# SSD mixer of a hybrid block: y summed in PSUM, squares reduced in one instruction, mask clamps and norm products moved

## The chip, the cores and the metric

The kernel runs on 1 core of one Trainium2 chip. The metric is device time in microseconds. The kernel before takes 1947.79 us, the median of 3 runs (1946.84 to 1948.59). Engines are named as in the profile: PE is TensorE, DVE is VectorE, ACT is ScalarE, POOL is GpSimd, SP is SyncE. ACT and SP also issue the DMA transfers that stand in their queues.

## What is computed

One decoder block on 1024 positions of 1024 channels, in float32: a projection `P = rmsnorm(x) @ W_in`, a gated short convolution, a Mamba-2 mixer (SSD, with 32 heads of 64 in 4 groups, chunks of 128 positions), a gated merge, and a convolutional MLP. The change lies in the SSD mixer:

```python
cb = einsum("bclgn,bcsgn->bcgls", cc, bc)
y_diag = einsum("bcgjls,bcsgjp->bclgjp", cb[:, :, :, None] * decay_in, x_)
y_off  = einsum("bclgn,bcgjpn,bcgjl->bclgjp", cc, prev, exp(a_cum))
y = y_diag + y_off + d_skip * xh
yf = y * silu(z)                                        # per group of 512 channels
yf = yf * rsqrt(mean(yf * yf, axis=-1) + EPS)           # then the norm's weight, W_s_out
```

`decay_in` is the exponential of differences of a cumulative sum, masked to the lower triangle.

## The kernel before

The large matrix products are made in pairs of column blocks, by a scheme of seven half-size products instead of eight (`Pair`, L274 on, and `then`, L368). Every operand is split into a rounded high part (`h_...`, an ACT cast, L146) and a low part (`l_...`, a subtraction on DVE or POOL, L147), so one half-size product is 12 matmuls of 128x512 on PE (`product`, L261, L268). A pair keeps one PSUM bank open through several of its products: after each, ACT copies the sum so far out (`u2...`, `u3...`, `cc`, L311 and L331), and only then may PE go on adding into that bank. `mark["act"]` holds the last such copy, `mark["pe"]` the last matmul of a product.

Beside the projection's pairs (`BESIDE`) runs the SSD mixer, from about 230 to 900 us of the span. Each finished product is a tick of a clock (`tick`, L394). `ssd_chunk` (L720) is a generator for one chunk of one group, 32 in all, started 6 ticks apart (`DSTEP`). `STAGES` says at which tick, counted from its diagonal block, each part of a chunk is written: loads (`m`, the rows of negated cumulative sums, and `in`, with x, B and C) at -9, the mask's clamps and exponential at -6 (`DECAY`, L742 and L743), transposes at -4 (`TRANS`, L748 to L770), z at -3, the diagonal block at 0 (`DIAG`, L788 to L821), squares at 3 (L824 to L828), the norm's product and, after each fourth chunk, its transpose at 6 (`NORM`, L831 to L844).

The names: `m` is first the load, then the mask (8 heads of 128x128), then mask times C·B (`pc`, in a bank of its own, made triangular into `cb`, L769, then L770 on DVE); `px` and `pb` hold x and B transposed; `bk` is ACT's copy of `pb` (L767); `pd` is the diagonal block, `po` the part from the carried state `st`, `pst` the new state; `xt` is x in the tile `in`, scaled by the skip on POOL (L763); DVE sums y in `xt` (L802, L805) and multiplies it into `zt` (L821). ACT squares `zt` into `eb` (L824); DVE adds the four blocks of 128 in two steps (L826, L828) into `ss`; PE sums over partitions (`pn`, L831), DVE scales (`yss`, L833), POOL takes the power -0.5 (`yr`, L837), and after four chunks PE transposes `yr` into `pr` (L841), ACT copies it to `rr` and SP stores it.

PSUM has 8 banks: four in rotation for `mm_tile` (the pairs' open sums) and four for `sd_tile`, which `px`, `pb`, `pc`, `pd`, `po`, `pst`, `pn`, `pr` and the pairs' second product `pb21` share. A tile taken from a rotation waits until the tile that had the bank four takings earlier has been read.

The order on each engine is not the order in which the code is written: a scheduler with a timeline of its own orders the instructions, and `tc.issue_after(i)` holds those written under it behind instruction `i`. The three engines' queues and the DMA queues then run in the order so fixed.

## Time and profile before

| | |
|---|---|
| median of 3 runs | 1947.79 us (1946.84 to 1948.59) |
| the profiled execution | 1947.18 us |
| its span, first to last instruction | 1945.5 us |
| PE busy | 1907.6 us (98%) |
| DVE busy | 1280.5 us (66%) |
| POOL busy | 1238.5 us (64%) |
| ACT busy | 958.6 us (49%) |
| mean granted PE clock | 0.995 of full speed |

The profile is of one execution. The span leaves out some 1.7 us around the program. PE is busy for all but 37.9 us of the span, so what counts is where PE stands idle and what ends each such wait; the share of busy time of the other engines says only how much room their queues have. A wait is put down to the instruction that came last.

### The profile page before, as it was taken

The numbers are of one execution on the slowest core, as the hardware profiler recorded it, in microseconds if no ns is written. First come the engines' busy times: TensorE is split into PE (matmuls) and PEld (weight loads), VectorE is DVE, ScalarE is ACT, GpSimd is POOL, SyncE is SP. The second block draws the span as 40 slices with busy tenths as digits, with TensorE's granted clock in tenths as the row PEclk, the third lists the DMA queues.
The fourth block names the chain that finished last, engine by engine and source line by source line (L and its number), as shares of the span: only waits on it lengthen the run. The fifth ranks groups of instructions, "written<-read, shape, count | busy, mean of one in ns | idle before, by whom it ended". The sixth has DMA issues, their size and how long they took to land.

```text
span 1945.5 us, 25405 instructions
## 1 busy us (share of the span) xinstructions
PE 1907.6 (98%) x8990; PEld 1567.3 (81%) x8990; DVE 1280.5 (66%) x1431; ACT 958.6 (49%) x1630; POOL 1238.5 (64%) x915
## 2 busy tenths in 40 slices
PE   8899999999999999999999999999999999999998
PEld 6788887787788778888888888887888888878886
DVE  9665567777786777777764833379655555675555
ACT  6347566667546754443542323454444444453334
POOL 8668766766767766766444534449867687754332
PEclk9999999999999999999999999999999999999999
DMA  4233354555545553443998974451332435487663
GB/s 157 87 95 134 132 168 147 179 158 164 184 138 160 170 166 124 149 144 122 386 368 275 358 253 164 160 178 65 109 114 76 128 131 174 143 290 257 203 195 141
DMA packets 180033, 337.90 MB, mean 174 GB/s; under 512 B 15265, under 2 KB 87745, under 8 KB 178882
## 3 DMA queue, kind: packets, MB, share of 16 engines
q1 hardware_dynamic: 93122, 253.43, 38.0%
q10 hardware_dynamic: 86784, 82.85, 13.2%
q8 instruction: 70, 1.15, 0.2%
q14 instruction: 57, 0.47, 0.1%
HBM read 246.82 MB, written 89.41 MB: 173 GB/s over the span
## 4 chain that ended last, share of the span: by engine, by line
PE 83%; DVE 5%; ACT 4%; DMA 3%; issue 3%; POOL 2%; ACTq 1%; SPq 0%; POOLq 0%; DVEq 0%
PE pb11up L268 9%; PE so L268 9%; PE pb11xb L268 6%; PE pt1up L268 5%; PE ya L268 5%; PE pb11cv L268 4%; PE pb11z L268 4%; PE d L1178 3%; PE d L1180 3%; PE d L1179 3%; PE pb21up L268 2%; PE pt1xb L268 2%; PE pb11ba L268 2%; PE pt1cv L268 2%; PE pt1g L268 2%
## 5 line engine op out<-in xcount | busy, mean ns | idle before, releaser
L618 DVE SCALAR_TENSOR_TENSOR cv<-xbc,scw,cv 128x1024 f32<-128x1024 f32 x72 | 121.9, 1696 | 42.4 <-ACT cv L614 41.1
L618 DVE SCALAR_TENSOR_TENSOR h<-fci,fcw,h 128x1024 f32<-128x1024 f32 x44 | 85.3, 1938 | 73.8 <-ACT h L614 73.2
L742 ACT ACTIVATE m<-m,tk 128x128 f32<-128x128 f32 x256 | 78.9, 390 | 87.3 <-DMA m<-acd 79.0
L147 POOL TENSOR_TENSOR l_ws<-raw_ws,h_ws 128x512 fp32r<-128x512 f32 x32 | 46.1, 1440 | 72.2 <-PE so L268 45.3
L146 ACT CAST h_ws<-raw_ws 128x512 fp32r<-128x512 f32 x64 | 39.8, 623 | 97.8 <-PE so L268 64.5
L268 PE MATMUL so<-yh,h_ws 128*128 128x512 f32 x256 | 69.0, 391 | 0.0
L268 PE MATMUL so<-yl,h_ws 128*128 128x512 f32 x256 | 68.6, 389 | 0.0
L268 PE MATMUL so<-yh,l_ws 128*128 128x512 f32 x256 | 68.5, 389 | 0.0
L146 ACT CAST h_wo<-raw_wo 128x512 fp32r<-128x512 f32 x48 | 29.7, 620 | 59.5 <-PE wo L1008 32.9
L147 DVE TENSOR_TENSOR l_ws<-raw_ws,h_ws 128x512 fp32r<-128x512 f32 x32 | 25.5, 796 | 50.9 <-PE so L268 21.4
L147 POOL TENSOR_TENSOR l_wo<-raw_wo,h_wo 128x512 fp32r<-128x512 f32 x24 | 31.7, 1322 | 39.4 <-PE wo L1008 31.3
L826 DVE TENSOR_TENSOR eb<-eb 128x256 f32<-128x256 f32 x32 | 27.4, 856 | 44.5 <-ACT eb L824 44.5
L268 PEld LDWEIGHTS so<-yh,l_ws 128*128 128x128 f32 x256 | 48.1, 188 | 10.0
L268 PEld LDWEIGHTS so<-yl,h_ws 128*128 128x128 f32 x256 | 48.1, 188 | 10.0
L268 PEld LDWEIGHTS so<-yh,h_ws 128*128 128x128 f32 x256 | 47.8, 188 | 9.6
L1155 DVE TENSOR_TENSOR h<-h 128x1024 f32<-128x1024 f32 x22 | 47.1, 2140 | 10.3 <-ACT h L1154 10.1
L314 DVE TENSOR_TENSOR fci<-fci,pb21up 128x512 f32<-128x512 f32 x18 | 12.4, 688 | 60.7 <-PE pb21up L268 60.7
L147 POOL TENSOR_TENSOR l_t3up<-raw_2up,h_t3up 128x512 fp32r<-128x512 f32 x22 | 31.2, 1418 | 32.1 <-PE pb11up L268 32.1
L1007 PE MATMUL wo<-l_wo,mh 128*128 128x512 f32 x128 | 50.0, 391 | 0.0
L1006 PE MATMUL wo<-h_wo,mh 128*128 128x512 f32 x128 | 50.0, 392 | 0.0
L1008 PE MATMUL wo<-h_wo,ml 128*128 128x512 f32 x128 | 49.7, 391 | 0.0
L770 DVE TENSOR_TENSOR m<-m,cb 128x1024 f32<-128x1024 f32 x32 | 48.6, 1518 | 0.6
(1127 smaller groups left out, 6527.8 us busy)
## 6 DMA issues: line engine op xcount, KB each, us to landing
m<-acd ACTq DMA_DIRECT2D x32, 512.0 KB, 3.9
raw_ws<-in_w_s_out SPq DMA_DIRECT2D x32, 512.0 KB, 4.7
ssd_in<-cv ACTq DMA_DIRECT2D x24, 512.0 KB, 2.9
in<-ssd_in ACTq DMA_DIRECT2D x32, 384.0 KB, 3.8
raw_wo<-in_w_o SPq DMA_DIRECT2D x24, 512.0 KB, 3.7
wd<-in_w_down SPq DMA_DIRECT2D x22, 512.0 KB, 7.0
td<-wd SPq DMA_DIRECT2D x44, 256.0 KB, 4.2
raw_2up<-in_w_up SPq DMA_DIRECT2D x22, 512.0 KB, 3.5
```

The source lines that it names most:

```text
L146: act.copy(hi, v)
L147: (eng or pool).tensor_tensor(lo, v, f32(hi), op=ALU.subtract)
L268: mark["pe"] = pe.matmul(ps, wt[:, k, :], ct[:, k, :], start=(start and n == 0), stop=(stop and n == 11), skip_group_check=held,).ins
L618: dve.scalar_tensor_tensor(cv, ci[:, j : j + SEQ], w[:, j : j + 1], cv, op0=ALU.mult, op1=ALU.add)
L742: act.activation(m[:, h, :], m[:, h, :], AF.Relu, bias=a)
L770: dve.tensor_tensor(m, m, cb.unsqueeze(1).to_broadcast([P, HG, P]), op=ALU.mult)
L1006: pe.matmul(pss[t], mh, wh, start=k == 0, stop=False)
L1007: pe.matmul(pss[t], mh, wl, start=False, stop=False)
L1008: pe.matmul(pss[t], ml, wh, start=False, stop=k == NK - 1)
L1178: pe.matmul(ps, aa[0][:, ts], bb[0], start=k == 0, stop=False)
L1179: pe.matmul(ps, aa[0][:, ts], bb[1], start=False, stop=False)
L1180: pe.matmul(ps, aa[1][:, ts], bb[0], start=False, stop=k == KF - 1)
```

## The change

- `y` is summed in the bank of its diagonal block, `pd += xt`, `pd += eb`, and read from there by `zt = pd * zt`. Before, it was summed in `xt`.
- `pb` and `pc` share one bank, `pbc`. The product with the triangle is made in place in it, and the mask is multiplied by it there. The tile `cb` is gone.
- One `tensor_reduce` over the four blocks takes the place of the two additions behind the square.
- The clamps and the exponential are written under `behind("act")`: on ACT they stand behind the pairs' last copy.
- The norm's product moves from tick 6 to 8, the power is taken once for four chunks, on 4 columns (8 instead of 32 instructions on POOL), and the transpose moves to tick 10. Both matmuls are written under `behind("pe")`.

```diff
@@ -49,7 +49,7 @@
 
 
 D0, DSTEP = 17, 6
-STAGES = LOAD_M, LOAD_IN, DECAY, TRANS, LOAD_Z, DIAG, SQUARES, NORM = -9, -9, -6, -4, -3, 0, 3, 6
+STAGES = LOAD_M, LOAD_IN, DECAY, TRANS, LOAD_Z, DIAG, SQUARES, NORM, ROW = -9, -9, -6, -4, -3, 0, 3, 8, 10
 
 
 AHEAD = 300
@@ -396,6 +396,13 @@
             clock[0] += 1
             for f in slots.pop(clock[0], ()):
                 f()
+
+    def behind(*engines):
+
+        held = ExitStack()
+        for e in engines:
+            held.enter_context(tc.issue_after(mark[e]))
+        return held
 
 
     xd_ = [dram.tile([P, 10, SEQ], F32, name=f"ssd_in{g}") for g in range(NG)]
@@ -737,18 +744,19 @@
         xt, bt, ct = inp[:, 0:4, :], inp[:, 4, :], inp[:, 5, :]
         yield
 
-        for h in range(HG):
-            a = tk[:, 0, cc, q, g * HG + h : g * HG + h + 1]
-            act.activation(m[:, h, :], m[:, h, :], AF.Relu, bias=a)
-        act.activation(m, m, AF.Exp, scale=-1.0)
+        with behind("act"):
+            for h in range(HG):
+                a = tk[:, 0, cc, q, g * HG + h : g * HG + h + 1]
+                act.activation(m[:, h, :], m[:, h, :], AF.Relu, bias=a)
+            act.activation(m, m, AF.Exp, scale=-1.0)
         yield
 
         px = sd_tile(f"px{nm}")
         for j in range(4):
             pe.transpose(px[:, j * P : (j + 1) * P], xt[:, j, :], ident)
-        pb = sd_tile(f"pb{nm}")[:, :P]
+        pbc = sd_tile(f"pbc{nm}")
+        pb, pc = pbc[:, :P], pbc[:, P : 2 * P]
         pe.transpose(pb, bt, ident)
-        pc = sd_tile(f"pc{nm}")[:, :P]
         pe.matmul(pc, bt, ct, start=True, stop=True)
         xd = c2(f"xd{nm}")
         dve.tensor_tensor(
@@ -765,9 +773,8 @@
         )
         bk = ssp.tile([P, P], F32, tag="bk", name=f"bk{nm}", bufs=1)
         act.copy(bk, pb)
-        cb = ssp.tile([P, P], F32, tag="cb", name=f"cb{nm}", bufs=1)
-        dve.tensor_tensor(cb, pc, tri, op=ALU.mult)
-        dve.tensor_tensor(m, m, cb.unsqueeze(1).to_broadcast([P, HG, P]), op=ALU.mult)
+        dve.tensor_tensor(pc, pc, tri, op=ALU.mult)
+        dve.tensor_tensor(m, m, pc.unsqueeze(1).to_broadcast([P, HG, P]), op=ALU.mult)
         yield
 
         eb = c2(f"eb{nm}")
@@ -799,10 +806,11 @@
         if c < NCH - 1:
             pst = sd_tile(f"pst{nm}")
             pe.matmul(pst, bk, xe, start=True, stop=True)
-        dve.tensor_tensor(xt, xt, tiles(pd), op=ALU.add)
+
+        dve.tensor_tensor(tiles(pd), tiles(pd), xt, op=ALU.add)
         if st is not None:
             dve.tensor_tensor(eb, po, eb, op=ALU.mult)
-            dve.tensor_tensor(xt, xt, tiles(eb), op=ALU.add)
+            dve.tensor_tensor(pd, pd, eb, op=ALU.add)
         if c < NCH - 1:
             if st is None:
                 st = states[g] = ssp.tile([P, HALF], F32, tag="st", name=f"st{g}", bufs=1)
@@ -818,30 +826,36 @@
                 cdb[:, q1, hsl, c1 : c1 + 1].to_broadcast([P, HG, HD]), op=ALU.mult,
             )
 
-        dve.tensor_tensor(zt, xt, zt, op=ALU.mult)
+        dve.tensor_tensor(zt, tiles(pd), zt, op=ALU.mult)
         yield
         sq = eb
         act.activation(sq, zt.rearrange("p j l -> p (j l)"), AF.Square)
         act.dma_start(yd[g, c // 4][:, :, hts], zt)
-        dve.tensor_tensor(sq[:, : 2 * P], sq[:, : 2 * P], sq[:, 2 * P :], op=ALU.add)
         sums = ssp.tile([P, P], F32, tag="ss", name=f"ss{nm}", bufs=1)
-        dve.tensor_tensor(sums, sq[:, :P], sq[:, P : 2 * P], op=ALU.add)
+        dve.tensor_reduce(
+            sums, sq.rearrange("p (j l) -> p l j", j=4), axis=mybir.AxisListType.X, op=ALU.add
+        )
         yield
         pn = sd_tile(f"pn{nm}")[:, :1]
-        pe.matmul(pn, sums, ones[:, :1], start=True, stop=True)
-        rs = tiny(f"yss{nm}")
-        dve.tensor_scalar(rs, pn, 1.0 / HALF, EPS, op0=ALU.mult, op1=ALU.add)
+        with behind("pe"):
+            pe.matmul(pn, sums, ones[:, :1], start=True, stop=True)
         if c % 4 == 0:
             stats[g, c // 4] = tiny(f"yr{nm}", 4)
         r = stats[g, c // 4]
-        pool.tensor_tensor(r[:, c % 4 : c % 4 + 1], rs, nhalf, op=ALU.pow)
+        dve.tensor_scalar(
+            r[:, c % 4 : c % 4 + 1], pn, 1.0 / HALF, EPS, op0=ALU.mult, op1=ALU.add
+        )
         if c % 4 == 3:
+            pool.tensor_tensor(r, r, nhalf.to_broadcast([P, 4]), op=ALU.pow)
+            yield
 
             pr = sd_tile(f"pr{nm}")[:4, :P]
-            pe.transpose(pr, r, ident)
+            with behind("pe"):
+                pe.transpose(pr, r, ident)
             rr = ssp.tile([P, P], F32, tag="ss", name=f"rr{nm}", bufs=1)
             act.copy(rr[:4, :], pr)
             sp.dma_start(rd[g, c // 4].rearrange("(c p) -> c p", c=4), rr[:4, :])
+        yield
         yield
 
     def at(n, f):
```

How this moves instructions, at three places. First ACT, around the copy `u2xb18` of the pair xb18 (chunk 3 of group 0 on PE). Before, the exponential of the mask `m0_4` and, five rows further up, its eight clamps stand ahead of the copy:

```order
L743 ACTIVATE m0_4_2777<-m0_4_2777 128x1024
L146 CAST h_b21g8_2899<-raw_1g8_2878 128x512
L781 DMA zt0_4_2966<-ssd_in0_84 128x4x128
L331 COPY z6_2408<-pb11z6_2412 128x512
L146 CAST h_t4xb18_2942<-raw_1xb18_2632 128x512
L776 DMA eb0_3_2772<-ead_109 64x4x128
L767 COPY bk0_3_2744<-pb0_3_2735 128x128
L776 DMA eb0_3_2772<-ead_109 64x4x128
L644 ACT_TABLE_LOAD
L644 ACTIVATE z6_2408<-z6_2408 128x1024
L645 DMA ssd_in1_85<-z6_2408 128x1024
L331 COPY u2xb18_2750<-pb11xb18_2634 128x512
```

Now:

```order
L146 CAST h_b21g8_2879<-raw_1g8_2858 128x512
L788 DMA zt0_4_2946<-ssd_in0_84 128x4x128
L331 COPY z6_2403<-pb11z6_2407 128x512
L146 CAST h_t4xb18_2923<-raw_1xb18_2622 128x512
L651 ACTIVATE z6_2403<-z6_2403 128x1024
L783 DMA eb0_3_2757<-ead_109 64x4x128
L775 COPY bk0_3_2731<-pbc0_3_2723 128x128
L783 DMA eb0_3_2757<-ead_109 64x4x128
L652 DMA ssd_in1_85<-z6_2403 128x1024
L331 COPY u2xb18_2736<-pb11xb18_2624 128x512
L750 ACTIVATE m0_4_2762<-m0_4_2762,tk_242 128x128 x8
L146 CAST h_t2g8_2954<-t2g8_2918 128x512
```

The clamps of `m0_4` and its exponential stand behind the copy, and one of the table loads ahead of it is gone.

Second PE, around the transpose `pr2_3` for the first four chunks of group 2. Before, `pn` (the norm's product) is followed by 29 matmuls of products, then `pr`:

```order
L268 MATMUL pb21g12_6053<-ua12l_145,h_b21g12_6054 128x512 x4
L268 MATMUL pb21g12_6053<-ua12h_144,l_b21g12_6055 128x512 x4
L831 MATMUL pn2_3_6112<-ones_119,ss2_3_6041 128x1
L268 MATMUL pb11xb14_5793<-ua22h_327,h_t4xb14_6078 128x512 x4
L268 MATMUL pb11xb14_5793<-ua22l_328,h_t4xb14_6078 128x512 x4
L268 MATMUL pb11xb14_5793<-ua22h_327,l_t4xb14_6079 128x512 x4
L268 MATMUL pb11g12_6021<-us2h_331,h_t2g12_6096 128x512 x4
L268 MATMUL pb11g12_6021<-us2l_332,h_t2g12_6096 128x512 x4
L268 MATMUL pb11g12_6021<-us2h_331,l_t2g12_6097 128x512 x4
L268 MATMUL pt1xb14_5962<-us4h_335,h_b22xb14_6155 128x512 x4
L268 MATMUL pt1xb14_5962<-us4l_336,h_b22xb14_6155 128x512
L841 MATMUL pr2_3_6117<-ident_75,yr2_0_5532 4x128
```

Now:

```order
L841 MATMUL pn2_3_6097<-ones_119,ss2_3_5945 128x1
L756 MATMUL px2_5_6101<-ident_75,in2_5_5954 128x128 x4
L759 MATMUL pbc2_5_6106<-ident_75,in2_5_5954 128x128
L760 MATMUL pbc2_5_6106<-in2_5_5954 128x128
L268 MATMUL pb11g12_5926<-us3h_333,h_t3g12_6119 128x512 x4
L268 MATMUL pb11g12_5926<-us3l_334,h_t3g12_6119 128x512 x4
L268 MATMUL pb11g12_5926<-us3h_333,l_t3g12_6120 128x512 x4
L268 MATMUL pb11cv2_6155<-ua11h_142,h_b11cv2_6156 128x512 x4
L268 MATMUL pb11cv2_6155<-ua11l_143,h_b11cv2_6156 128x512 x4
L268 MATMUL pb11cv2_6155<-ua11h_142,l_b11cv2_6157 128x512 x4
L268 MATMUL pt1cv2_6312<-us1h_329,h_t1cv2_6313 128x512 x3
L854 MATMUL pr2_3_6172<-ident_75,yr2_0_5522 4x128
```

`pn` stands ahead of the next but one chunk's transposes instead, and 27 matmuls of products lie between it and `pr`. Over the eight such places there are 22 to 36 before and 24 to 40 now.

Third PE, between the C·B product and the diagonal block of chunk 3 of group 2. Before, `pc2_3` stands three rows above the first of these, with eight matmuls between:

```order
L268 MATMUL pb21xb14_5830<-ua12h_144,l_b21xb14_5832 128x512 x4
L268 MATMUL pb11z14_5572<-ua22h_327,h_t4z14_5869 128x512 x4
L268 MATMUL pb11z14_5572<-ua22l_328,h_t4z14_5869 128x512 x4
L268 MATMUL pb11z14_5572<-ua22h_327,l_t4z14_5870 128x512 x4
L268 MATMUL pt1z14_5714<-us4h_335,h_b22z14_5904 128x512 x4
L268 MATMUL pb11xb14_5793<-us2h_331,h_t2xb14_5887 128x512 x4
L268 MATMUL pb11xb14_5793<-us2l_332,h_t2xb14_5887 128x512 x4
L268 MATMUL pb11xb14_5793<-us2h_331,l_t2xb14_5888 128x512 x4
L268 MATMUL pt1z14_5714<-us4l_336,h_b22z14_5904 128x512 x4
L268 MATMUL pt1z14_5714<-us4h_335,l_b22z14_5905 128x512 x4
L831 MATMUL pn2_2_5920<-ones_119,ss2_2_5850 128x1
L788 MATMUL pd2_3_5925<-m2_3_5660,xd2_3_5819 64x128 x8
```

Now, from `pbc2_3` on:

```order
L759 MATMUL pbc2_3_5727<-ident_75,in2_3_5576 128x128
L760 MATMUL pbc2_3_5727<-in2_3_5576 128x128
L268 MATMUL pb21xb14_5740<-ua12h_144,h_b21xb14_5741 128x512 x4
L268 MATMUL pb21xb14_5740<-ua12l_145,h_b21xb14_5741 128x512 x4
L268 MATMUL pb21xb14_5740<-ua12h_144,l_b21xb14_5742 128x512 x4
L268 MATMUL pb11xb14_5702<-us2h_331,l_t2xb14_5797 128x512 x4
L268 MATMUL pt1z14_5628<-us4h_335,h_b22z14_5813 128x512 x4
L268 MATMUL pt1z14_5628<-us4l_336,h_b22z14_5813 128x512 x4
L268 MATMUL pt1z14_5628<-us4h_335,l_b22z14_5814 128x512 x4
L268 MATMUL pt1xb14_5866<-us1h_329,h_t1xb14_5867 128x512
L795 MATMUL pd2_3_5829<-m2_3_5574,xd2_3_5730 64x128 x8
```

There were 48 matmuls of products between `pc` and `pd`, now there are 29. Over the 32 chunks the smallest counts were 26, 29, 30, 30, 36 and 37, and are now 29, 31, 33, 37 and 38; from the next on, 43 or more before and 45 or more now.

## Rows read from the trace of the kernel before

**Rows 1.** The page's first line.
```profile
span 1945.5 us, 25405 instructions
```

**Rows 2.** Two stretches: length; busy PE, PEld, DVE, ACT, POOL; PE clock; DMA share; GB/s.
```profile
230.00:900.00 670.00, 658.24 (x3435) 535.83 (x3434) 497.95 (x589) 391.32 (x736) 473.45 (x360) 1.00 0.49 155
900.00:1945.00 1045.00, 1033.05 (x4565) 852.43 (x4563) 626.13 (x662) 439.67 (x675) 595.66 (x423) 1.00 0.57 198
```

**Rows 3.** PE's waits, 230 to 900 us: for whom, us, times, longest.
```profile
PE pb11xb L268 <- ACT u2xb L331: 2.8, 2, 1.6
PE pr L841 <- POOL yr L837: 2.4, 3, 1.8
PE pb11cv L268 <- ACT u2cv L331: 1.8, 1, 1.8
PE pt1g L268 <- DVE gt L346: 1.5, 1, 1.5
PE pb11cv L268 <- ACT cc L311: 1.3, 1, 1.3
PE pb11xb L268 <- ACT u3xb L331: 0.9, 1, 0.9
PE pn L831 <- DVE ss L828: 0.8, 1, 0.8
PE pb11g L268 <- ACT u3g L331: 0.2, 1, 0.2
```

**Rows 4.** PE's timeline: start, us, instruction, count, and idle time before it.
```profile
311.48 1.07 PE L268 MATMUL pt1xb<-us1l,h_t1xb 128*128 128x512 f32 x4
312.39 1.07 PE L268 MATMUL pt1xb<-us1h,l_t1xb 128*128 128x512 f32 x4
314.64 1.20 PE L268 MATMUL pb11xb<-us3h,h_t3xb 128*128 128x512 f32 x4 [1.18 <-ACT u2xb L331]
...
344.98 0.27 PE L841 MATMUL pr<-ident,yr 128*4 128x128 f32 x1 [1.81 <-POOL yr L837]
```

**Rows 5.** ACT's timeline around two of the copies.
```profile
312.53 1.06 ACT L644 ACTIVATE z<-z 128x1024 f32<-128x1024 f32 x1
...
314.00 0.58 ACT L331 COPY u2xb<-pb11xb 128x512 f32<-128x512 f32 x1 [0.41 <-ACT z L644]
...
700.46 0.40 ACT L742 ACTIVATE m<-m,tk 128x128 f32<-128x128 f32 x1 [4.14 <-DMA m<-acd]
...
707.17 0.58 ACT L331 COPY u2cv<-pb11cv 128x512 f32<-128x512 f32 x1
```

**Rows 6.** ACT's longest wait, 230 to 900 us, as in rows 3.
```profile
ACT m L742 <- DMA m<-acd: 79.0, 21, 7.4
```

**Rows 7.** POOL's timeline at the first transpose of the norm.
```profile
343.97 0.95 POOL L837 TENSOR_TENSOR yr<-yss,nhalf 128x1 f32<-128x1 f32 x1
```

**Rows 8.** DVE's groups, 230 to 910 us: busy us, mean ns | idle before.
```profile
L770 DVE TENSOR_TENSOR m<-m,cb 128x1024 f32<-128x1024 f32 x32 | 48.6, 1518 | 0.6
L805 DVE TENSOR_TENSOR in<-in,eb 128x512 f32<-128x512 f32 x28 | 27.8, 991 | 0.7
L826 DVE TENSOR_TENSOR eb<-eb 128x256 f32<-128x256 f32 x32 | 27.4, 856 | 44.5 <-ACT eb L824 44.5
L828 DVE TENSOR_TENSOR ss<-eb 128x128 f32<-128x128 f32 x32 | 24.6, 768 | 1.5 <-DMA rd<-rr 0.8
L802 DVE TENSOR_TENSOR in<-in,pd 128x512 f32<-128x512 f32 x32 | 21.8, 681 | 19.3 <-PE pd L788 10.8 <-POOL raw_1cv L323 4.3 <-issue 1.7
L769 DVE TENSOR_TENSOR cb<-pc,tri 128x128 f32<-128x128 f32 x32 | 8.9, 278 | 0.0
```

**Rows 9.** One stretch at the lower PE clock, columns as in rows 2.
```profile
709.30:712.70 3.40, 3.40 (x10) 2.63 (x9) 3.40 (x2) 1.29 (x4) 2.56 (x2) 0.50 0.53 157
```

**Rows 10.** PE's and ACT's timelines, chunk 6 of group 2.
```profile
701.08 0.39 PE L752 MATMUL pc<-in 128*128 128x128 f32 x2
...
708.16 0.27 ACT L767 COPY bk<-pb 128x128 f32<-128x128 f32 x1
```

## The prediction

> **What bounds the kernel now.** I read the three stretches first. PE is busy nearly all of the span [rows 1, 2], so the change can save only time in which PE stands idle or runs at a lower clock: it takes no matmul away. Between 230 and 900 us, where the SSD mixer runs, PE is busy 658.24 of 670.00 us, that is idle for 11.8 us [rows 2]. The list of PE's waits in that stretch accounts for all of it: 2.8 + 2.4 + 1.8 + 1.5 + 1.3 + 0.9 + 0.8 + 0.2 = 11.7 us, in eleven waits [rows 3]. Three kinds are to be seen there. Six waits, 7.0 us (`u2xb` twice, `u2cv`, `cc`, `u3xb`, `u3g`), are for ACT's copy of a pair's open sum. Four, 3.2 us, are for the norm (`yr` from POOL three times, `ss` from DVE once). One, 1.5 us, is for a sum on DVE (`gt`). Outside the waits PE keeps one step: four matmuls of 128x512 every 0.91 us, 0.227 us each [rows 4]. [...] So the most that the named causes can give is 11.7 + 1.7 = 13.4 us.
>
> The rest of the span lies outside the reach: the change touches the SSD part alone, and PE's instructions stand in the same order from the first matmul of `ya`, at some 900 us, to the end. All sums below are made against the profiled execution, 1947.2 us; the median of the runs, 1947.8 us, is 0.6 us above it. I take what is saved in the profile off the median.
>
> **Clamps behind the copies.** Before, ACT's queue holds the eight clamps soon after the mask's load has been issued, so ACT waits for the load: 79.0 us in 21 waits, the longest 7.4 us [rows 6]. While it waits it copies no sum for PE. The `u2cv` place shows it: ACT waits 4.14 us for `m` at 700.46, does clamps, exponential and others, and comes to the copy at 707.17; PE waits 1.8 us [rows 3, 5]. At `u2xb` no such wait is near, but the clamps, two table loads and an exponential stand in the ACT rows ahead of the copy, then the silu of z at 312.53; the copy starts at 314.00, and PE waits 1.18 us [rows 4, 5]. In the new order the clamps stand behind the copy and belong to a mask whose load was issued about a chunk earlier. No instruction is added. The DMA issues in ACT's queue remain where they were relative to the copies, but one row is new among them: the next `in` load now waits for DVE's `pd += xt`, with the copies queued behind it. That wait ends earlier than the one that it replaces, which was for the last read of `xt` two additions later. I credit 5.8 of the 7.0 us: at the places of `u2cv` and `u3xb` another function's work still stands ahead of the copy, and I leave 1.2 us there. Bounds: 0 to 7.0.
>
> **The norm.** The wait of `pn` for `ss` (0.8 us) should go: the product moves two ticks, some 24 matmuls or 5.4 us, away from the squares [rows 3, 4]. The three waits of `pr` are for POOL: at the first, POOL comes to the power at 343.97, behind other work in its queue, and PE waits 1.81 us [rows 4, 7]. The transposes were meant to move away too, but the order gives little: 22 to 36 matmuls between `pn` and `pr` before, 24 to 40 now, 31.6 for 27.9 on the mean, which is 3.7 x 0.227 = 0.8 us. So the power can still be late at a place or two. 24 powers of one column leave POOL; no row has a power of 128x4, which I bound by the longest row of a POOL power, 0.95 us [rows 7], below and four times that above. I credit 1.6 of 2.4 us, bounds 0 to 2.4; four such powers' worth of lateness, 2.9 us at one place, would be the worst. The ROW part's copy `rr`, one small ACT copy, waits in the new order for the next chunk's `pn`, since `rr` and `ss` share one buffer; what stands behind it is one or two copies. It lies ahead of no PE instruction within 7 us of matmuls, so nothing for it.
>
> **DVE.** Every addition with both inputs in SBUF that comes to read one from PSUM gets shorter by what the rows show: 681 ns for `in<-in,pd` against 991 for `in<-in,eb`, the same shape [rows 8]. The mask's product, 1518 ns, comes down to at most twice 681. The two steps of the squares, 856 + 768 ns, become one reduction, for which there is no row; I bound it by 512 elements at the price of `in<-in,pd`, 681 ns, below, and by the two that it replaces above. Taken at the lower ends that is 0.3 + 0.2 + 0.9 us a chunk, and some 0.4 for the multiplication into `zt`: about 1.8 us of 15 a chunk. In-place results in PSUM have no row either; from nothing to the 310 ns that separate the two rows. None of it is on PE's path by itself. It gives the 1.5 us of `gt`, which waits in a crowded DVE queue, and I credit it whole because PE's order also puts `pd` and `po` ahead of the matmul that waited.
>
> [...]
>
> **A new wait.** `bk` and the C·B product now share a bank, so DVE's product with the triangle, and behind it the mask's product and all that stands after them in DVE's queue, wait for ACT's copy of `bk`. Before they waited for PE alone. How late ACT can be: `pc` at 701.08, the copy done at 708.43, 7.35 us [rows 10]. Add the triangle, 0.28, and the mask, 1.52 [rows 8]: 9.15 us from `pc` to a mask that `pd` can use. PE's own cover is the matmuls between the two: 48 at most chunks, 10.9 us, enough. At five chunks there are 29, 31, 33, 37 and 38, that is 6.6, 7.0, 7.5, 8.4 and 8.6 us, and `pd` would wait 2.6 + 2.1 + 1.7 + 0.8 + 0.5 = 7.7 us if ACT were as late as that at each. The other end is zero: before, six chunks have 26 to 37 matmuls there, and PE has no wait for the mask [rows 3]. I take 2.4 us, nearer to that end.
>
> **The clock.** The stretch at half clock [rows 9] comes 1.5 us behind the `u2cv` wait, and the wait for `gt` stands some 17 us ahead of that. If both go I expect it to go: 1.7 us, bounds 0 to 1.7.
>
> **Sum.** 5.8 + 0.8 + 1.6 + 1.5 + 1.7 - 2.4 = 9.0 us. 1947.8 - 9.0 = **1938.8 us**. Everything credited and nothing new: 1947.8 - 13.4 = 1934.4.
>
> **Rivals.**
> - *The copies stay late.* Table loads, silu and exponential remain in ACT's queue, and any of them can stand ahead of a copy. Then the 5.8 and the clock's 1.7 stay: 1938.8 + 7.5 = 1946.3. For it: at `u2xb` the last ahead of the copy is a silu. Against: ACT is idle 42% of the stretch [rows 2], much of it for `m`.
> [...]
> - *Given back later.* PE reaches 900 us some 9 us earlier, and the weights that the next stage streams (198 GB/s, DMA share 0.57 [rows 2]) or the store of `rd` in SP's queue, with loads queued behind it, become late: up to all of it, 1947.5. Against: PE is idle 12 us in 1045 there now, and none of the waits is for a load.
> - *The mask comes too late: slower.* The exponential is moved back by up to a chunk and has to be done before the mask's product. From the last thing that ACT's queue needs of PE before it, to `pd`, PE has at least 75 matmuls in the new order, 17 us. Copy, eight clamps, table load and exponential are about 6 us, triangle and mask 1.8, which leaves 9. From there on each us that ACT is late is a us of PE. ACT's longest wait now is 7.4 us [rows 6]; with two such in a row, 2 us too late at eight chunks, it would cost 16 us: 1938.8 + 16 = 1954.8.
>
> **How the numbers follow.** Forecast 0.58, copies late 0.16, DVE no lighter 0.10, given back 0.08, mask too late 0.08. A measurement of this kernel can tell about 0.2%, 3.9 us, from no change: faster is below 1943.9, slower above 1951.7. Faster: 0.58 + 0.10 = 0.68. Same: 0.16 + 0.08 = 0.24. Slower 0.08. The range goes from all that is on offer, 1934.4, rounded down to 1934, past the copies' rival to 1946.5; outside are the last two rivals, 0.16.
>
> **What would show it.** The waits of PE between 230 and 900 us should sum to 3 to 5 us, without `u2xb` and `pn`; ACT's wait for `m` should be a few us in place of 79; no stretch at half clock near 700 us; DVE busy some 50 us less in all. Against me: waits of `pd` for the mask (`m`), waits for `u2`, `u3` or `cc` as long as now, or new waits after 900 us.

## The result, and the profile after

The changed kernel takes 1936.07 us (median of 4 runs, 1934.58 to 1937.09), the kernel before, beside it, 1948.19 us: a ratio of 0.994, with a 95% interval of 0.9929 to 0.9952. That is 12.1 us less; 9.0 were forecast. The profiled execution took 1937.09 us and spans 1935.4, 10.1 less than that of before. Medians here and below are of all runs, but the ratios leave out two runs at another pace (one with the clamps alone, 3204.56 us at a granted clock of 0.557, and one of the kernel before, 4947.40 us), and a ratio need not be the quotient of two medians.

The same stretch as in [rows 2], columns as there:

```profile
230.00:900.00 670.00, 667.94 (x3485) 540.11 (x3484) 440.20 (x567) 404.96 (x762) 426.64 (x344) 1.00 0.49 157
```

Of 670.00 us PE is now idle for 2.06, where it was idle for 11.76. DVE has 57.8 us less to do, POOL 46.8 us less. What is left of PE's list, as in [rows 3]:

```profile
PE pb11xb L268 <- ACT u3xb L331: 1.5, 1, 1.5
PE pt1g L268 <- DVE gt L346: 0.4, 1, 0.4
```

Six of the eight rows of [rows 3] are gone, the waits for `u2xb`, `u2cv`, `cc`, `u3g`, `yr` and `ss`; `gt` went from 1.5 to 0.4 us, and `u3xb` from 0.9 to 1.5. No stretch at half clock is left between 230 and 900 us. On PE the first transposes of the SSD part and the first `ya` stand 681.83 us apart here and 693.47 before. First the two rows of before, then those of now:

```profile
244.58 0.60 PE L748 MATMUL px<-ident,in 128*128 128x128 f32 x4
...
938.05 1.07 PE L268 MATMUL ya<-tah,h_wa 128*128 128x512 f32 x4
```

```profile
244.36 0.60 PE L756 MATMUL px<-ident,in 128*128 128x128 f32 x4
...
926.19 1.07 PE L268 MATMUL ya<-tah,h_wa 128*128 128x512 f32 x4
```

So the stretch that the change touches gives 11.6 us. From `ya` to the end this execution needs 1.8 us more (1009.17 us for 1007.41), for most of it at one wait that was not there before:

```profile
PE pt_v L185 <- DVE h L1046: 1.4, 1, 1.4
```

ACT's row of [rows 6], the 79.0 us in which it waited for the load of `m`, has no counterpart. At the only late copy, PE's wait of 1.50 us for `u3xb`, ACT stood at another load. The chain of waits there, followed back from PE (start, us, what), and then ACT's rows:

```profile
649.12 6.12 DMA yd<-zt
...
655.32 0.38 ACTq L788
```

```profile
655.32 0.38 ACTq L788 DMA_DIRECT2D zt<-ssd_in  x1
...
656.32 0.58 ACT L331 COPY u3xb<-pb11xb 128x512 f32<-128x512 f32 x1
```

The load of the next z (`zt<-ssd_in`) goes into the buffer of the chunk before last, whose store (`yd<-zt`) was issued at 649.12 and needs 6.12 us. ACT did not pass the load in its own queue: it stood idle for 5.46 us ahead of the cast at 655.79, and the cast and the copy behind the load are some 5 us late.

### The profile page after: what moved, and what is told of

Read it like the earlier page. It is cut to its first block, busy times and chain, and to the rows that moved or that the text cites. A ratio compares the mean times of both kernels' runs of the same rounds, so it can differ in the third digit from the quotient of the medians.

```text
span 1935.4 us, 25341 instructions
## 1 busy us (share of the span) xinstructions
PE 1905.1 (98%) x8990; PEld 1560.6 (81%) x8990; DVE 1213.3 (63%) x1399; ACT 959.3 (50%) x1628; POOL 1185.7 (61%) x891
## 3 DMA queue, kind: packets, MB, share of 16 engines
q10 hardware_dynamic: 86784, 82.85, 13.4%
q8 instruction: 70, 1.15, 0.3%
## 4 chain that ended last, share of the span: by engine, by line
PE 90%; DVE 3%; ACT 2%; DMA 2%; issue 2%; POOL 1%; ACTq 0%; SPq 0%; POOLq 0%; DVEq 0%
PE pb11up L268 9%; PE so L268 9%; PE pb11xb L268 6%; PE pt1up L268 6%; PE pb11cv L268 5%; PE ya L268 5%; PE pb11z L268 4%; PE d L1192 3%; PE d L1193 3%; PE d L1194 3%; PE pt1xb L268 3%; PE pb11g L268 3%; PE pb21up L268 2%; PE pt1cv L268 2%; PE pb11ba L268 2%; PE pt1z L268 2%
## 5 line engine op out<-in xcount | busy, mean ns | idle before, releaser
L824 POOL TENSOR_TENSOR sn<-st,cdb 128x512 f32<-128x512 f32 x24 | 27.2, 1134 | 50.9 <-DVE st L819 43.5
L268 PEld LDWEIGHTS so<-yl,h_ws 128*128 128x128 f32 x256 | 48.1, 188 | 10.1
L771 POOL TENSOR_TENSOR in<-in,dsk 128x512 f32<-128x512 f32 x32 | 38.2, 1194 | 18.1 <-PE px L756 18.1
```

Source lines behind the costliest of these rows:

```text
L268: mark["pe"] = pe.matmul(ps, wt[:, k, :], ct[:, k, :], start=(start and n == 0), stop=(stop and n == 11), skip_group_check=held,).ins
```

## The experiments

All times are medians, ratios are to the kernel before on the same chip, with their 95% intervals. "Idle" is PE's idle time between 230 and 900 us, 670.00 less PE's busy time in the row of that stretch.

### Each part alone, and the change without one part

The change has three parts: the clamps (C) behind the copies, the norm (N) at its later ticks with one power, and DVE's part (D: y in PSUM, the shared bank, the reduction). Six kernels hold the other combinations. Their edits are the hunks of the diff above. Besides the helper `behind`, C is the first hunk here, N the next two, D the rest (with the tile `cb` and the banks as in the diff above); the kernels without a part have the same lines turned round:

```diff
+        with behind("act"):
-        for h in range(HG):
+            for h in range(HG):
...
-STAGES = LOAD_M, LOAD_IN, DECAY, TRANS, LOAD_Z, DIAG, SQUARES, NORM = -9, -9, -6, -4, -3, 0, 3, 6
+STAGES = LOAD_M, LOAD_IN, DECAY, TRANS, LOAD_Z, DIAG, SQUARES, NORM, ROW = -9, -9, -6, -4, -3, 0, 3, 8, 10
...
-        pool.tensor_tensor(r[:, c % 4 : c % 4 + 1], rs, nhalf, op=ALU.pow)
+            pool.tensor_tensor(r, r, nhalf.to_broadcast([P, 4]), op=ALU.pow)
...
-        dve.tensor_tensor(xt, xt, tiles(pd), op=ALU.add)
+        dve.tensor_tensor(tiles(pd), tiles(pd), xt, op=ALU.add)
...
-        dve.tensor_tensor(sums, sq[:, :P], sq[:, P : 2 * P], op=ALU.add)
+        dve.tensor_reduce(
```

C alone. 

> The kernel before with one edit: the eight clamps and the exponential are written behind the pairs' last copy on ACT. The theory of the prediction (each part takes away the waits that were put to it): the six waits for u2, u3 and cc go but for some 1 us, PE's idle time in the SSD stretch falls from 11.8 us to about 6, the stretch at half clock goes or stays with the gt wait, time 1940 to 1942.5 for the 1948.2 of before; ACT's 79 us of waits for the load of m fall to a few. Rival, lighter queues (what helps is that DVE and POOL have less to do, and the copies are late because what feeds them is late): at most 2 us less, 1946 or more, and waits for u2, u3 or cc remain. Rival, another order (any edit moves the schedule and the waits fall elsewhere by chance): PE's idle time stays at 9 to 14 us, under other names.

N alone. 

> The kernel before with one edit: the norm's product at tick 8 and its transpose at tick 10, both behind the last product on PE, and one power on POOL for four chunks. The theory of the prediction: the waits of pn for ss and of pr for yr go, 3.2 us, the others stay: 1945.0, PE's idle time in the SSD stretch 8 to 9 us. Rival, lighter queues: the 24 powers that leave POOL take 20 us of its work away, and products that wait for operands from POOL come earlier too: 1943 or less. Rival, another order: the idle time stays at 9 to 14 us under other names.

D alone. 

> The kernel before with y summed in the bank of its diagonal block, B's transpose and the C.B product in one bank, and the squares reduced in one instruction; the order of the clamps and of the norm as before. The theory of the prediction: DVE's work in the SSD stretch falls by 45 to 60 us, but on PE only the wait for gt goes, 1.5 us, with perhaps the 1.7 us of half clock: 1945 to 1946.7; the waits for u2, u3 and cc stay, 5 us or more. Rival, lighter queues: this part makes most of the gain, 1941 or less. Rival, another order: idle time 9 to 14 us under other names.

The change without C. 

> The changed kernel with the clamps and the exponential written as before, not behind the last copy. The theory of the prediction: the copies are late again, 5 to 7 us of waits for u2, u3 and cc come back, and ACT waits some 79 us for the load of m: 1941 to 1943.5 for the 1936.1 of the changed kernel. Rival, lighter queues: with less on DVE and POOL the copies are in time anyway: 1938 or less.

The change without N. 

> The changed kernel with the norm as before: product at tick 6, a power per chunk on POOL, the transpose at once. Theory after the first runs (PE's waits are in series: a family of waits that is left grows when another is taken away, because PE comes earlier to a source that is as late as ever; the three parts together do more than their sum): the waits of pn for ss and of pr for yr come back, 3 to 4.5 us, the copies stay in time, PE's idle time in the SSD stretch is 4 to 6 us; since the norm's move alone made PE's own work there 2.9 us longer, some of that comes back: 1936 to 1939. Rival, the parts just add: clamps alone gave 5.1 us and DVE's part alone 4.0, so 1939.5 or more.

The change without D. 

> The kernel before with the clamps behind the copies and the norm moved, but y, the C.B product and the squares on DVE as before. Theory of waits in series: the copies are in time, pn and pr do not wait, the wait for gt stays, 1.5 to 2 us, perhaps one for the mask; idle time 3 to 5 us in the SSD stretch, PE's own work as long as in the run with the norm alone: 1939 to 1942. Rival, the parts just add: 5.1 us less and 0.5 us more, 1944. Rival, DVE is what decides: its 50 us more of work make u2, u3 or gt wait, idle time 7 us or more, 1943 or more.

Measured, with ACT's waits for the load of `m` at the clamps (the row `m<-acd` of its list):

| parts | idle, us | ACT for `m`, us | median, us | ratio |
|---|---|---|---|---|
| none | 11.76 | 79.0 | 1948.19 to 1949.47 | 1 |
| C | 7.81 | none | 1943.51 | 0.9977 (0.9966 to 0.9988) |
| N | 11.96 | 70.2 | 1949.09 | 1.0002 (0.9992 to 1.0013) |
| D | 10.57 | 65.3 | 1944.56 | 0.9982 (0.9974 to 0.9991) |
| N and D | 13.54 | 94.8 | 1952.00 | 1.0012 (1.0003 to 1.0021) |
| C and D | 5.04 | none | 1937.88 | 0.9943 (0.9931 to 0.9956) |
| C and N | 5.93 | none | 1943.67 | 0.9975 (0.9964 to 0.9986) |
| all | 2.06 | none | 1936.07 | 0.9940 (0.9929 to 0.9952) |

Against what was expected: with C alone the idle time was to be about 6 us and is 7.81, and the time lies 1.0 us above its range. N alone was to take 3.2 us off and takes none. D alone lies just below its range, with 8.1 us of waits for copies where 5 or more were expected. Without C the kernel is 8.5 us slower than the range allowed, because the waits for copies come to 11.7 us and not to 5 to 7. C and N lie 1.7 us above their range. Only C and D came out as expected, and there too PE still waits 2.1 us for copies (`cc` and `u3xb`) and not at all for `ss`.

In PE's idle time the parts do not add. Alone they change it by -3.95, +0.20 and -1.19 us, together 4.94 less; all three in one kernel give 9.70, each from one profiled execution. In the ratios the three parts alone come to 0.39% and the whole change to 0.60%, which the intervals barely tell apart. Every kernel with C is idle for 7.81 us or less and every one without it for 10.57 or more. The rows show how. PE's waits with C alone:

```profile
PE pr L850 <- POOL yr L846: 2.4, 1, 2.4
PE pn L840 <- DVE ss L837: 1.9, 2, 1.5
PE pt1g L268 <- DVE gt L346: 1.8, 1, 1.8
```

The waits for `u2xb`, `u2cv`, `cc` and `u3xb` are gone, as forecast (1.0 us for another copy, `u3z`, is new). But `ss` went from 0.8 to 1.9 us and `gt` from 1.5 to 1.8, and the norm's 2.4 us are there again, in one wait instead of three: what is not treated stays or grows here. With N alone it is less plain. The two waits for `u2xb` are gone without C, while other copies and new waits for banks take their place:

```profile
PE pb11cv L268 <- ACT u2cv L331: 2.6, 1, 2.6
PE pb11cv L268 <- ACT cc L311: 1.8, 1, 1.8
PE pc L760 <- DVE st L819: 1.5, 2, 0.8
```

That is what the rival "another order" had: idle time of 9 to 14 us under other names. N alone (11.96) fits it, D alone (10.57) does not rule it out; for C it falls (7.81). The plainest case of a wait that grows is with D alone, at the place of [rows 4]. Before, PE waited 1.18 us for `u2xb` there and went on at 314.64. Now:

```profile
314.64 1.19 PE L268 MATMUL pb11xb<-us3h,h_t3xb 128*128 128x512 f32 x4 [1.54 <-ACT u2xb L331]
```

PE comes 0.36 us earlier, waits 0.36 us longer, and goes on at the same 314.64. The mirror of C alone is the change without C:

```profile
PE pb11xb L268 <- ACT u2xb L331: 4.4, 2, 3.0
PE pb11cv L268 <- ACT u2cv L331: 3.2, 1, 3.2
...
PE pd L794 <- DVE m L776: 1.4, 2, 1.1
```

```profile
ACT m L749 <- DMA m<-acd: 94.8, 26, 6.8
```

`ss`, `yr` and `gt` are gone, and the two waits for `u2xb` went from 2.8 to 4.4 us, the one for `u2cv` from 1.8 to 3.2, while ACT waits longer for `m` than before. With the clamps where they were, PE is tied to a loop that N and D do not touch: the load of `m` is issued when PE's diagonal block has freed the tile, it lands some 4 us later (4.2 in the middle, by this run's page, in its list of DMA issues; 3.9 by that of before), and the copies that PE needs stand behind that load's clamps. That the loop is what fixes the pace is argued from these rows, not shown by a run of its own. What is shown: on top of N and D, C is worth 11.5 us of idle time, alone 4.0; D on top of C is worth 2.8, on C and N 3.9, alone 1.2; N is worth 3.0 on top of C and D, 1.9 on top of C, and without C it adds 0.2 alone and 3.0 on top of D. The rival "lighter queues" falls with N and D together (1952.0): less work on DVE and POOL by itself made the copies no less late. "The parts just add" falls with N and D, whose parts alone give a ratio of 0.9984 and which together measure 1.0012. C and D, at 1937.88 for a price of 1939.5 or more, speak against it too, but less surely: 0.9959 by the parts, 0.9943 measured, with intervals about as wide as the difference. For C and N the sum had 1944, and 1943.67 was measured: there the rival came out, and the theory's 1939 to 1942 did not.

### The price of DVE's operations

> Not the block but the prices alone: each form of the DVE work eight times with POOL idle and eight times beside a row of 128x512 additions on POOL; it leaves the whole block out. Theory (an operation of DVE with both inputs in SBUF takes as long as one that reads PSUM when POOL is idle, and is held up by POOL when it works; one that reads PSUM is not): addition of 128x512 from SBUF 690 ns beside an idle POOL and over 1000 beside a busy one, from PSUM 680 to 700 in both, in place in PSUM the same; mask product 1215 and over 1700 from SBUF, 1215 and 1215 with the factor in PSUM; the strided reduction 1070 in both, the two additions 700 together and over 1500. Rival (a PSUM input is cheaper by itself): 300 ns between the additions with POOL idle too. [...]

```diff
+            dve.tensor_tensor(vo, vo, va, op=ALU.add)
...
+            dve.tensor_tensor(vo, px, vo, op=ALU.add)
...
+            dve.tensor_tensor(py, py, vo, op=ALU.add)
...
+    for _ in range(110):
+        pool.tensor_tensor(full[:, 2, :HALF], pq, full[:, 2, :HALF], op=ALU.add)
```

The names with v are tiles in SBUF, `px` and `py` lie in PSUM.

DVE's groups with POOL idle (shapes, count, busy us, mean ns):

```profile
L120 DVE TENSOR_TENSOR vm<-vm,vc 128x1024 f32<-128x1024 f32 x8 | 9.7, 1218 | 0.0
L123 DVE TENSOR_TENSOR vm<-vm,px 128x1024 f32<-128x1024 f32 x8 | 9.7, 1211 | 0.0
L126 DVE TENSOR_REDUCE vs<-vo 128x128 f32<-128x512 f32 x8 | 8.1, 1016 | 0.2
L117 DVE TENSOR_TENSOR py<-py,vo 128x512 f32<-128x512 f32 x8 | 5.5, 693 | 0.0
L114 DVE TENSOR_TENSOR vo<-px,vo 128x512 f32<-128x512 f32 x8 | 5.5, 691 | 0.3
L136 DVE TENSOR_REDUCE vs<-px 128x128 f32<-128x512 f32 x8 | 5.5, 691 | 0.3
L129 DVE TENSOR_REDUCE vs<-vo 128x128 f32<-128x512 f32 x8 | 5.5, 686 | 0.3
L111 DVE TENSOR_TENSOR vo<-vo,va 128x512 f32<-128x512 f32 x8 | 5.5, 685 | 0.0
L132 DVE TENSOR_TENSOR vt<-vo 128x256 f32<-128x256 f32 x8 | 3.4, 424 | 0.2
L133 DVE TENSOR_TENSOR vs<-vt 128x128 f32<-128x128 f32 x8 | 2.3, 292 | 0.3
```

The same beside POOL's row of additions:

```profile
L120 DVE TENSOR_TENSOR vm<-vm,vc 128x1024 f32<-128x1024 f32 x8 | 18.2, 2277 | 0.0
L111 DVE TENSOR_TENSOR vo<-vo,va 128x512 f32<-128x512 f32 x8 | 12.9, 1611 | 0.0
L132 DVE TENSOR_TENSOR vt<-vo 128x256 f32<-128x256 f32 x8 | 11.2, 1404 | 0.2
L123 DVE TENSOR_TENSOR vm<-vm,px 128x1024 f32<-128x1024 f32 x8 | 9.7, 1211 | 0.0
L133 DVE TENSOR_TENSOR vs<-vt 128x128 f32<-128x128 f32 x8 | 8.9, 1116 | 0.3
L126 DVE TENSOR_REDUCE vs<-vo 128x128 f32<-128x512 f32 x8 | 8.2, 1027 | 0.2
...
L114 DVE TENSOR_TENSOR vo<-px,vo 128x512 f32<-128x512 f32 x8 | 5.5, 689 | 0.2
```

With POOL idle an addition of 128x512 takes 685 ns from SBUF and 691 with one input in PSUM; in place in PSUM 693. Beside POOL the one from SBUF takes 1611 ns and the one from PSUM 689. The mask's product: 1218 and 1211 idle, 2277 and 1211 beside POOL. It is POOL, not the bank, that made 991 of 681 in [rows 8]. The trace of before holds this already, in the least, middle and greatest time of the 28 additions:

```profile
L805 DVE TENSOR_TENSOR in<-in,eb x28: 677/856/1812, 278.6 to 902.0; 128x512 f32<-128x512 f32 x28
```

Eight of them ran with no POOL instruction beside them and took 691 to 693 ns; twelve ran wholly beside POOL and took 1173 in the mean. The 32 with one input in PSUM took 666 to 689. The rival falls: with POOL idle there are 6 ns between the two, not 300. The strided reduction is 1016 and 1027; the two additions that it replaces are 424 + 292 = 716 idle and 1404 + 1116 beside POOL. So with an idle POOL the reduction is the dearer one by 300 ns. From PSUM the same reduction takes 691, and a reduction along adjacent elements in SBUF 686.

In the changed kernel the groups answer to [rows 8] so:

```profile
L777 DVE TENSOR_TENSOR m<-m,pbc 128x1024 f32<-128x1024 f32 x32 | 38.9, 1216 | 0.7
L835 DVE TENSOR_REDUCE ss<-eb 128x128 f32<-128x512 f32 x32 | 34.6, 1080 | 16.4 <-DMA rd<-rr 12.3 <-ACT eb L832 4.1
...
L829 DVE TENSOR_TENSOR zt<-pd,zt 128x512 f32<-128x512 f32 x32 | 21.9, 685 | 0.4
...
L813 DVE TENSOR_TENSOR pd<-pd,eb 128x512 f32<-128x512 f32 x28 | 19.5, 697 | 0.8
```

The product into `zt` had this row in the trace of before:

```profile
L821 DVE TENSOR_TENSOR zt<-in,zt 128x512 f32<-128x512 f32 x32 | 36.1, 1128 | 0.3
```

With its 1128 ns, and 856 + 768 for the squares, a chunk has 0.30 + 0.29 + 0.44 + 0.54 = 1.6 us less, where the prediction had 1.8.

### y in SBUF, and two banks

The changed kernel with y summed in `xt`:

```diff
-        dve.tensor_tensor(tiles(pd), tiles(pd), xt, op=ALU.add)
+        dve.tensor_tensor(xt, xt, tiles(pd), op=ALU.add)
...
-            dve.tensor_tensor(pd, pd, eb, op=ALU.add)
+            dve.tensor_tensor(xt, xt, tiles(eb), op=ALU.add)
...
-        dve.tensor_tensor(zt, tiles(pd), zt, op=ALU.mult)
+        dve.tensor_tensor(zt, xt, zt, op=ALU.mult)
```

> The changed kernel with y summed in xt in SBUF as before. By the measured prices (685 ns for an addition from SBUF beside an idle POOL, 1611 beside a busy one, 690 from PSUM in both) DVE gets the 20 to 25 us back that the part saved, and POOL gets longer rows too. Theory: DVE has 34% idle time, so of that little reaches PE: 0 to 3 us, as waits for gt, the mask or a bank; 1936 to 1939. Rival, DVE decides: 4 us or more back, 1940 or more.

It takes 1941.71 us, 0.9963 (0.9949 to 0.9976); idle 5.00 us. DVE has 20.2 us more to do (460.36 for 440.20), as expected, and on the same chip the changed kernel takes 1937.56, so 4.1 us come back, of which 2.7 are idle time (2.28 in that run of the changed kernel). The waits are eight small ones, the longest two:

```profile
PE pb11xb L268 <- ACT xbc L311: 1.2, 1, 1.2
PE pd L795 <- DVE m L777: 1.2, 1, 1.2
```

So DVE's lighter queue does matter once the clamps are out of the way, though DVE is idle a third of the stretch. By the idle time the theory's 0 to 3 us hold; by the median its range up to 1939 is missed, and the rival's 4 us, 1940 or more, is met. The two are not clearly told apart, and the 1.4 us that no idle time shows are open.

Two banks instead of one:

```diff
-        pbc = sd_tile(f"pbc{nm}")
-        pb, pc = pbc[:, :P], pbc[:, P : 2 * P]
+        pb = sd_tile(f"pb{nm}")[:, :P]
...
+        pc = sd_tile(f"pc{nm}")[:, :P]
...
-        dve.tensor_tensor(pc, pc, tri, op=ALU.mult)
-        dve.tensor_tensor(m, m, pc.unsqueeze(1).to_broadcast([P, HG, P]), op=ALU.mult)
...
+        dve.tensor_tensor(cb, pc, tri, op=ALU.mult)
+        dve.tensor_tensor(m, m, cb.unsqueeze(1).to_broadcast([P, HG, P]), op=ALU.mult)
```

> The changed kernel with B's transpose and the C.B product in two banks, and the product with the triangle in the tile cb again, so that DVE's product no longer waits for ACT's copy of bk. In the changed kernel DVE stands 10.5 us in seven waits at that place, and PE none at pd; the mask is ready 0.3 us ahead of pd at the closest chunk. Theory (the wait is hidden, the prediction's 2.4 us for it were too much): DVE's wait goes, PE does not come earlier for it; one more bank a chunk is taken from the four, so waits of pc or px for a bank come, as in the run with clamps and norm alone (3.4 us): 1936 to 1941. Rival (the shared bank costs what the prediction took): 2 us or more faster than the changed kernel.

It takes 1942.10 us, 0.996 (0.9946 to 0.9975), slower than the changed kernel by 4.5 us and 1.1 above the range; 3.0 of them are idle time. First the wait of DVE in the changed kernel, then two of PE's with two banks:

```profile
DVE pbc L776 <- ACT bk L775: 10.5, 7, 2.7
```

```profile
PE pd L796 <- DVE m L778: 1.8, 3, 1.1
PE pb21z L268 <- ACT rr L857: 1.3, 1, 1.3
```

DVE's 10.5 us at the shared bank cost PE nothing. Without the shared bank `pd` waits 1.8 us for the mask, whose product takes its factor from SBUF again (1518 ns that way in [rows 8], 1216 from the shared bank), and `pb21z`, `px` and `pc` wait 2.6 us for banks. The rival, 2 us faster, falls.

### The load of z

> The changed kernel with the gated product written into the tile of xd, squared and stored from there, so that the tile of z is free when DVE has read it and not when the store has landed. In the changed kernel ACT stands 24.0 us in nine waits at the load of the next z, 5.0 us at the longest, right ahead of the one late copy, u3xb, for which PE waits 1.5 us. Theory (the late store of y holds the queue): ACT's waits at that load fall under 5 us, the wait for u3xb goes, PE's idle time in the SSD stretch is 0 to 1 us, 1934 to 1936. Rival, another wait takes its place: idle time as now, 2 us or more, 1936 or more.

> The changed kernel with the gated product in the tile of xd once more, to be compared with the changed kernel on the same chip. Theory: its 2 us of waits are gone, 1.5 to 3 us less than the changed kernel, 0.992 to 0.993 of the kernel before. Rival: the lower time of the first run was the chip's, and the two do not differ by 0.05%.

> The changed kernel once more, beside the next three on one chip. Expected: 0.993 to 0.995 of the kernel before; PE's idle time in the SSD stretch again about 2 us, with the wait for u3xb at the same place (the waits are set by the order and the durations, not by chance); the wait of 1.4 us before pt_v, at some 1300 us, and the stretches at half clock at the start and at some 1320 us come or go (chance), by 1.5 to 5 us in all. Rival: the wait before pt_v is the change's own, and is there again.

```diff
-        dve.tensor_tensor(zt, tiles(pd), zt, op=ALU.mult)
+        dve.tensor_tensor(xd, pd, zt.rearrange("p j l -> p (j l)"), op=ALU.mult)
...
-        act.activation(sq, zt.rearrange("p j l -> p (j l)"), AF.Square)
-        act.dma_start(yd[g, c // 4][:, :, hts], zt)
+        act.activation(sq, xd, AF.Square)
+        act.dma_start(yd[g, c // 4][:, :, hts], tiles(xd))
```

The first run takes 1934.64 us, 0.9931 (0.9918 to 0.9943). The second, 1935.08, 0.9928 (0.9912 to 0.9943), stands on one chip with the changed kernel's 1937.56, 0.9935 (0.992 to 0.995). The stretch of [rows 2] in the second run, and in the changed kernel run again:

```profile
230.00:900.00 670.00, 670.00 (x3499) 543.15 (x3498) 446.34 (x568) 405.60 (x763) 427.48 (x346) 1.00 0.50 157
```

```profile
230.00:900.00 670.00, 667.72 (x3485) 540.44 (x3485) 440.61 (x567) 404.64 (x762) 426.54 (x344) 1.00 0.50 156
```

PE is busy for 670.00 of 670.00 us (669.86 in the first run): every wait of the SSD part is gone. At the same place ACT and PE have the same order as in the changed kernel, but the load now follows the store at once, and the copy is in time. In the first run:

```profile
645.11 0.55 ACTq L833 DMA_DIRECT2D yd<-xd  x1
...
645.72 0.89 ACTq L788 DMA_DIRECT2D zt<-ssd_in  x1
...
648.17 0.58 ACT L331 COPY u3xb<-pb11xb 128x512 f32<-128x512 f32 x1
```

The changed kernel run again has the same waits (idle 2.28, `u3xb` 1.6 us), and the wait before `pt_v` with 0.9. On that chip the version with the product in `xd` is 2.5 us below the changed kernel, and its idle time falls by 2.28 us. The intervals of the two ratios overlap, so the medians alone would not settle it; the rows of the stretch do, for the stretch. Its two medians are the lowest of this study.

## Why the prediction was right, and where not

**The bound and the stretch** held. What could be saved was PE's idle time between 230 and 900 us with the half clock in it, 13.4 us at most, and 11.6 came; the terms below sum to 5.5 + 3.2 + 1.1 + 1.7 = 11.5.

**The copies**: 5.8 credited of 7.0, and 5.5 came (1.5 us remain at `u3xb`). The named cause is confirmed by the run with C alone, in which all the copies of `u2xb`, `u2cv`, `cc` and `u3xb` are in time, and by the run without C, in which they are late again. The reserve of 1.2 us was for work of other functions ahead of a copy; what is really left is a load of z behind a store.

**The norm**: 0.8 + 1.6 credited, 0.8 + 2.4 came. The power of four columns that I bounded from 0.95 us up takes 1.15:

```profile
L849 POOL TENSOR_TENSOR yr<-yr,nhalf 128x4 f32<-128x4 f32 x7 | 8.0, 1149 | 3.2 <-DVE yr L845 3.1
```

**`gt`**: 1.5 credited, 1.1 came. The cause, a lighter DVE queue, fits the run with D alone, where this wait is gone; but it is gone with C and N as well, where DVE's work is 487.09 us and so hardly lighter. PE's longest wait in that kernel is another one:

```profile
PE pc L761 <- DVE xbc L314: 2.8, 1, 2.8
```

**The clock**: 1.7, came whole, but not for the reason given. The term is an estimate, half of the 3.40 us at a clock of 0.50 in [rows 9]; no run shows it by itself. Inside that stretch, in the trace of before, the four matmuls at 710.12 took 1.71 us up to the next ones, where four take 0.91 in [rows 4]:

```profile
710.12 1.91 PE L268 MATMUL pb11cv<-us3h,l_t3cv 128*128 128x512 f32 x4
711.83 1.27 PE L268 MATMUL pb21cv<-ua12h,h_b21cv 128*128 128x512 f32 x3
```

In the changed kernel the stretch is gone, and of the 11.6 us that came 9.7 are idle time. I tied it to the waits for `u2cv` and `gt`. With C and N both are gone, and yet a stretch of 3.41 us at half clock stands at 309.1 us, right behind that wait of 2.8 us for `xbc`.

**The new wait for the mask** is the term that was mis-sized: 2.4 us were taken off, and nothing was lost. No wait of `pd` stands in the list. I had made it from ACT's lateness at one place of before (7.35 us), when it still had clamps ahead of its copies. In the changed kernel the copy of `bk` is late by at most 2.7 us, and from the end of the mask's product to the start of `pd` there is time in all 32 chunks, 0.3 us at the closest. This is most of the difference between the 9.0 forecast and the 12.1 measured; in the profiled executions, 10.1, the loss of 1.8 us behind `ya` hides it. That loss does not show the rival "given back later". The wait before `pt_v` is there in both runs of the changed kernel (1.4 and 0.9 us) and in the second with the product in `xd` (0.7), but not in the first, where PE comes to it as early; and it is there without C (0.9), a kernel that is no faster than before. Two executions with the product in `xd` need 1007.36 and 1010.23 us from `ya` to the end, so 1.8 us lie within what executions of one kernel differ by.

**DVE**: the mechanism was wrong where the number was right. I read from two rows that an addition is 310 ns shorter with an input in PSUM. It is not: with POOL idle the addition takes 685 ns from SBUF and 691 with an input in PSUM, 6 ns more. Beside POOL's additions the one from SBUF is held up, 1611 ns, and the one with an input in PSUM is not, 689. DVE did get lighter, but my number for it was right by luck. A DVE that gets no lighter, for which I had a chance of 0.10, did not come: it has 57.8 us less to do.

**The sum** was made as if each term stood by itself. For the whole change that came out: all families of waits were treated at once. That this is why is argued from the rows above, not shown. For the parts it holds with C alone (5.8 us by my terms, 5.1 by the medians) and fails elsewhere: N alone was worth 2.4 us by my terms, and no change was measured; C and N were worth 8.2 and gave 5.8; N and D without C were worth 5.6 with the clock, 3.2 less the mask's wait, and are slower than before by 0.12%.

**The slower rival**, a mask that comes too late by the clamps' move, did not come. `pd` does not wait in the changed kernel; in other kernels it waits for the mask 0.4 us (N), 0.7 (D), 1.4 (N and D), 1.3 (C and N), 1.2 (y in SBUF) and 1.8 (two banks), far from the 16 that I had priced.

## What to carry to other kernels

When one engine is busy 98% of the time, list its waits by what they wait for, and treat all families in one change or judge the change by the list, not by the time: a family that is left can take up a good part of what another gives. Where a queue runs in order, as ACT's did here, ask of every load what frees its buffer: a load that waits for a store, or an operation that waits for a load, is paid for by whatever stands behind it (here a store of 6.12 us held ACT for 5.46 us and PE for 1.5). DVE's operations with two SBUF inputs were priced here by what POOL did beside them, an addition of 128x512 at 685 ns alone and 1611 beside POOL's, so look at the spread, not the mean; the spread of before, 677 to 1812 ns, would have warned me.

## What the runs showed of the hardware that I had not expected

- With POOL idle a strided sum of four blocks of 128 by one reduction took 1016 ns from SBUF and 691 from PSUM; along adjacent elements 686 from SBUF (512 elements each).
- PE's own time for the same matmuls is not the same in kernels that order them differently. Between the first transposes and the first `ya`, less the idle time and less an estimated 1.7 us where a stretch at half clock lies in it, the kernels need from 678.3 us (D alone) to 682.9 (N alone). That is 4.6 us that no wait shows, where two executions of one kernel differ by 0.5 (changed kernel) and 0.1 (product in `xd`); which neighbours cost it is open. The prediction had put nothing for it.
- In the SSD part six of the kernels have a stretch at half clock (0.50 before, 0.51 with C alone, 0.52 without C), five of them right behind their longest single wait, the kernel before behind its second longest. With C alone, for one, PE stood idle for 2.37 us ahead of `pr` at 346.52, and then:

```profile
347.20:350.70 3.50, 3.50 (x21) 2.84 (x18) 3.48 (x3) 2.01 (x5) 1.46 (x1) 0.51 0.88 311
```

  The kernels whose waits there are all short, the changed one among them (1.5 us at the longest), have none. Others, at the start, at 62 us and at some 1320 us, come and go from one execution to the next of kernels that do not differ there (at 0.50 from 1314.0 to 1320.5 us in the second run with the product in `xd`), by 1.7 to 3.4 us, half of their lengths; they are part of the spread of the times.
